# Ten activation tiles ahead in the room of four row slots, in a product-key expert kernel

## The chip, the cores and the metric

The kernel runs on one core of a Trainium2 chip. The metric is the device time of one execution in microseconds (us). The engines are named as the profile names them: PE (TensorE) with its weight loads PEld, DVE (VectorE), ACT (ScalarE), POOL (GpSimd) and SP (SyncE, which here issues most of the transfers).

## What is computed

The reference chains two blocks over 512 tokens of width 1024, in float32. Everything up to the last part (latent attention, then gated linear attention and sparse attention with top-k) is the same in both kernels and is not looked at here. The change is in the last part, a product-key expert layer (PEER) with 16384 experts:

```python
def _peer(h, w_q, sub_keys_1, sub_keys_2, expert_u, expert_v):
    q = (h @ w_q).reshape(B, S, PEER_HEADS, PEER_DKEY)
    s1, s2 = ...                                  # scores against 128 + 128 sub-keys
    v1, i1 = lax.top_k(s1, PEER_TOPK)             # 16 of each
    v2, i2 = lax.top_k(s2, PEER_TOPK)
    cand = v1[..., :, None] + v2[..., None, :]
    best, ci = lax.top_k(cand, PEER_TOPK)         # 16 of the 256 sums, for 8 heads
    expert_idx = ia * PEER_NKEYS + ib
    gates = jax.nn.softmax(best, axis=-1)
    u, v = expert_u[expert_idx], expert_v[expert_idx]
    a = gelu(einsum('td,thkd->thk', h, u)) * gates
    return einsum('thk,thkd->td', a, v)
```

## The kernel before

**Dense for three token tiles, sparse for the fourth.** Tokens come in four tiles of 128. For the first three (TD = 384 tokens) the layer is computed densely over all 16384 experts, in 128 steps j of 128 experts each. `a[j]` (128 experts x 384 tokens) is Gelu(u[j] h); `w` is a[j] times the gate matrix G, which is zero where an expert was not chosen; and w times v[j] (128 experts x 1024) adds to the result Y, which stays in six of eight PSUM banks. For the fourth tile, 128 tokens x 8 heads x 16 rows are gathered, 256 gathers of 128 rows in all: 128 of u (each reduced to one column by line 1166, output `junk`) and then 128 of v (each added into `spx` by line 1176).

**Products in three parts.** A float32 product is three matmuls: both operands are split into a rounded high part and the rest (`split`, lines 73 to 78). ACT writes the high part (`wh` from `wr` for u, from `vr` or `wr` for v, `wwh` from `w`; line 79), and DVE or POOL the rest (`wl`, `wwl`; line 81). One a tile is computed by an "a block" of 24 matmuls of 384 columns (lines 85 to 87), one step of Y by a "Y block" of 18 matmuls of 512 columns (lines 1254 to 1256). The split halves of u and v share three buffers (`wh`, `wl`, bufs=3), the raw u has two, the raw v two, w and its halves two each.

**The order of the stages.** (1) DVE chooses the experts of the first three tiles (`choose`, ending in line 1372), a long chain of 128x384 instructions. Meanwhile PE computes tiles of a ahead, with `pull`: each unit of eight is three matmuls, eight units a tile. Nineteen tiles stand here (`pull(8 * 19)`). For tiles computed ahead (`early`) the rest of the split is POOL's work. (2) PE transposes the chosen indices and gates (line 1097, output `T` by line 1099). (3) The one-hot stage: DVE and POOL write one-hot matrices `o1` and `o2` for four tokens at a time (lines 1107 and 1112), PE multiplies them (line 1125), ACT evicts the gates, and one unit of a (three matmuls) is pulled for each of 96 groups: twelve more tiles. One further tile is pulled at the end, 32 in all. (4) The expert loop, 128 steps.

**One step of the loop**, in the order of the code: `pull(8)` for the next a tile (its splits are now DVE's), `weights(j + 1)` (w, its split, the load and split of v[j + 1]), the Y block of step j, then at most two units of the fourth tile's choosing (steps 0 to 7, lines 1315 to 1378), and from step 7 on gathered rows. There are a tiles left to pull in steps 0 to 95; from step 96 on a step has only its Y block. The a tiles live in 29 buffers (NA + 1); a tile's Gelu (line 1036) waits for the w that reads the buffer's tile before.

**Gathered rows.** Eight row buffers of 128x1024 are used in turn: four in `more`, allocated when the choosing ends, and four in `rows`. `used(j)` spreads the 256 gathers over the steps 7 to 115, with three times the weight while a tiles are still pulled: two or three a step up to step 96, at most one after it.

**What sets the order.** PE follows the code's order throughout. In the loop DVE and POOL do too (`manual_schedule`). ACT's instructions and SP's transfers are put in order when the kernel is built, by a scheduler; on the chip each engine takes its instructions strictly in that order.

Of the kernel before, what the change touches and what calls it, by code (L numbers as in the profile page):

```python
# [9 lines left out]
F32 = mybir.dt.float32  # L10
# [15 lines left out]
TD = 384  # L26
NE = 16384
NA = 28
POOL_U = (3,)
POOL_A = True  # L30
LAG = 20
# [14 lines left out]
class Build:  # L46
# [961 lines left out]
    def phase_c(self, x3):  # L1008
        nc, i, tc, pc = self.nc, self.i, self.tc, self.pc
# [16 lines left out]
        def a_units(j):  # L1026

            wh, wl = au.pop(j, None) or self.wload(i["u"][j], [8, 128], early)
            ps = self.bank()
            for k in range(8):  # L1030
                self.mm3(ps[:, :TD], wh[:, k], wl[:, k], hh[:, k, :TD], hl[:, k, :TD], k == 0, k == 7)
                if k == 2 and early:
                    au[j + 1] = self.wload(i["u"][j + 1], [8, 128], True)
                yield
            a = pc.tile([128, TD], F32, name="a", tag="a", bufs=NA + 1)
            nc.scalar.activation(a, ps[:, :TD], AF.Gelu)  # L1036
            at[j] = a

# [35 lines left out]
        pr = self.es.enter_context(tc.tile_pool(name="pr", bufs=1, side="right", reuse_waits="tile"))  # L1074

        more = pr.tile([128, 4, 1024], F32, name="rows")
        early, au = True, {0: self.wload(i["u"][0], [8, 128], True)}

        def ahead():
# [5 lines left out]
        def pull(n):  # L1085
            for _ in range(n):
                next(al, None)
                self.pulled += 1

        with tc.tile_pool(name="p2", bufs=1, reuse_waits="tile") as p2:  # L1090
            ia, ib, gt = self.choose(0, NT, vals, idxs, p2)
            pull(8 * 19)
            Ts = []
            for tt in range(NT):
                ps = self.bank()
                for n, t in enumerate((ia, ib, gt)):
                    nc.tensor.transpose(ps[:, 128 * n:128 * n + 128], t[:, tt], self.ident)
                T = p2.tile([128, 3, 128], F32, name="T", tag="T", bufs=3)
                nc.scalar.activation(T, ps[:, :384].rearrange("p (n t) -> p n t", t=128), AF.Copy)
                Ts.append(T)  # L1100

            def one_hots(g):

                T, t0 = Ts[g // 32], 4 * (g % 32)
                o1 = p2.tile([128, 4, 128], F32, name="o1", tag="o1", bufs=3)
                o2 = p2.tile([128, 4, 128], F32, name="o2", tag="o2", bufs=3)
                nc.vector.tensor_tensor(o1, iota[:, None, :].to_broadcast([128, 4, 128]),
                                        T[:, 0, t0:t0 + 4].unsqueeze(2).to_broadcast([128, 4, 128]),
                                        op=OP.is_equal)
                for u in range(4):  # L1110
                    e = nc.gpsimd if u in POOL_U else nc.vector
                    e.tensor_scalar(o2[:, u], iota, T[:, 1, t0 + u:t0 + u + 1], T[:, 2, t0 + u:t0 + u + 1],
                                    op0=OP.is_equal, op1=OP.mult)
                return o1, o2

            oh = {0: one_hots(0)}
            for c in range(TD // 32):
                gb = self.xp.tile([128, 128, 32], F32, name="gb", tag="X")
                for g in range(8 * c, 8 * c + 8):
                    if g + 1 < TD // 4:  # L1120
                        oh[g + 1] = one_hots(g + 1)
                    o1, o2 = oh.pop(g)
                    ps = self.bank()
                    for u in range(4):
                        nc.tensor.matmul(ps[:, 128 * u:128 * u + 128], o1[:, u], o2[:, u], start=True, stop=True)
                    pull(1)
                    gs = 4 * (g % 8)
                    nc.scalar.activation(gb[:, :, gs:gs + 4].rearrange("p j t -> p t j"),
                                         ps.rearrange("p (t j) -> p t j", j=128), AF.Copy)
                nc.scalar.dma_start(out=gd[c], in_=gb)  # L1130
            spx = self.xp.tile([128, 4, 1024], F32, name="spx", tag="X")
            h2t, ysp, rep, fg = [spx[:, n] for n in range(4)]

            n = TD // 32 - 1
            G = {0: spx[:, 2:].rearrange("p n d -> p (n d)")[:, :4 * TD].rearrange("p (c t) -> p c t", t=128)}
            nc.sync.dma_start(out=G[0][:, :n], in_=gd[:n, :, :4].rearrange("c p j t -> p c (j t)"))
            nc.scalar.activation(G[0][:, n], gb[:, :4].rearrange("p j t -> p (j t)"), AF.Copy)
            pull(8)

        rows = self.xp.tile([128, 4, 1024], F32, name="rows", tag="X")  # L1140
        slots = [more[:, n] for n in range(4)] + [rows[:, n] for n in range(4)]
        for hf in range(2):
            ps = self.bank()
            for k in range(4):
# [5 lines left out]
        with tc.tile_pool(name="p3", bufs=1, reuse_waits="tile") as p3:  # L1150
# [3 lines left out]
            def gather(e):  # L1154

                table = i["u_rows"] if e < 128 else i["v"].rearrange("j p d -> (j p) d")
                r = slots[e % 8]
                ix = sidx[:, e // 128, e % 128:e % 128 + 1]
                nc.gpsimd.indirect_dma_start(out=r, out_offset=None, in_=table,  # L1159
                                             in_offset=bass.IndirectOffsetOnAxis(ap=ix, axis=0))  # L1160
                return e, r
# [63 lines left out]

            early = False
            NJ = NE // 128
            es, got, ready = 0, [], NJ - self.pulled // 8
            last = ready + LAG
            ch, first = choosing(), None  # L1230

            def used(j):

                share = [3 if k < ready else 1 for k in range(first, last)]
                return 256 * sum(share[:j - first]) // sum(share)
            pool_order = tc.manual_schedule(engines={mybir.EngineType.Pool, mybir.EngineType.DVE})
            pool_order.__enter__()
# [1 line left out]
            for j in range(NJ):  # L1239
                if j == 0:  # L1240
                    weights(0)
                pull(8)
                if j + 1 < NJ:
                    weights(j + 1)
                if j == NJ - 2:
                    continue
                for tt in range(NT):
                    ts_ = slice(128 * tt, 128 * tt + 128)
                    for jj in ((j,) if j < NJ - 2 else (j - 1, j)):
                        wh, wl, vh, vl = ws[jj]  # L1250
                        for n in range(2):
                            ns = slice(512 * n, 512 * n + 512)
                            y = Y[2 * tt + n]
                            nc.tensor.matmul(y, wh[:, ts_], vh[:, ns], start=(jj == 0), stop=False)  # L1254
                            nc.tensor.matmul(y, wh[:, ts_], vl[:, ns], start=False, stop=False)  # L1255
                            nc.tensor.matmul(y, wl[:, ts_], vh[:, ns], start=False, stop=(jj == NJ - 1))  # L1256
                ws.pop(j)
                for _ in range(2):
                    if first is None and next(ch, 0) == 0:
                        first = j  # L1260
                if first is not None:
                    while got and got[0][0] < used(j):
                        sparse(*got.pop(0))
                    while es < 256 and len(got) < 8:
                        got.append(gather(es))
                        es += 1
                if j == last:
                    xts = self.xp.tile([128, 4, 1024], F32, name="xts", tag="X")
                    f = i["final_g"]
                    nc.sync.dma_start(out=fg, in_=bass.AP(tensor=f.tensor, offset=f.offset, ap=[[0, 128], [1, 1024]]))  # L1270
                if 0 <= (j - last) // 2 < 4 and (j - last) % 2 == 0:
                    tt = 3 - (j - last) // 2
                    nc.sync.dma_start(out=xts[:, tt], in_=x3d[tt])
                if j == last + 2:
                    assert es == 256 and not got
                    for hf in range(2):
                        ps = self.bank()
                        for k in range(4):
                            dg = p3.tile([128, 128], F32, name="dg", tag="dg", bufs=1)
                            c = 40 + 4 * hf + k  # L1280
                            nc.vector.tensor_scalar(dg, self.ident, self.adac(c), None, op0=OP.mult)
                            nc.tensor.matmul(ps[:, 128 * k:128 * k + 128], self.ones, dg, start=True, stop=True)  # L1282
                        nc.scalar.activation(rep[:, 512 * hf:512 * hf + 512], ps, AF.Copy)
                if j == last + 4:
                    finish(3)
# [185 lines left out]
```

## Time and profile before

| | us |
|---|---|
| median of 3 runs (2253.89 to 2257.43) | 2256.93 |
| the profiled execution, its own time | 2257.13 |
| span of its trace | 2255.3 |
| PE busy in the span | 2131.9 (95%) |
| DVE busy | 1692.6 (75%) |
| ACT busy | 958.5 (42%) |
| POOL busy | 847.9 (38%) |

PE is the busiest engine, with a mean granted clock of 0.981 of full speed. Busy shares of the whole span hide that the stages have different limits, so the rows below are taken by stage. Times in them count from the span's start. In a row of the timeline the first number is the start, the second the duration; a bracket at the end says how long the engine sat idle before it and what released it. Matmuls overlap in the pipeline, so a block's length is read from start to start. `xN` at the end counts instructions merged into the row.

### The profile page before, as it was taken

To read this page: it belongs to the slowest core of one execution; us is meant where nothing else is said; L and a number is where in the kernel's file an instruction comes from. 1 tells how busy PE (TensorE), PEld (TensorE's weight loads), DVE (VectorE), ACT (ScalarE), POOL (GpSimd) and SP (SyncE) were. 2 spreads that over 40 slices of the span, in tenths; PEclk is the share of its full clock that TensorE was granted. 3 is DMA by queue.
4 is the path that set the end of the run, shared out by engine and by line. 5 is a ranking of instruction groups with operands and counts; after the bars stand their busy time and mean duration, and the time that the engine had idled before them with its cause. 6 is when DMAs were issued, how large, how long until landed. Compare 5 with 4: busy or idle time off the path is not lost. (4 is left out here: it accounts for less than half of the span.)

```text
span 2255.3 us, 31436 instructions
## 1 busy us (share of the span) xinstructions
PE 2131.9 (95%) x11443; PEld 1877.8 (83%) x11443; DVE 1692.6 (75%) x3304; ACT 958.5 (42%) x1429; POOL 847.9 (38%) x630
## 2 busy tenths in 40 slices
PE   8999999989999999999699889999999999999996
PEld 5778988877888889899688878888888888888875
DVE  6877348996667555879999678777777787877875
ACT  5376446344245533343477433333333333333332
POOL 4333330110056313335699224444444444444200
PEclk9999999999999999999899999999999999999998
DMA  6511223214822132233254659899899898899952
GB/s 249 182 48 63 79 82 112 90 57 132 274 89 66 66 107 91 93 124 120 99 202 197 227 177 333 303 322 319 307 320 312 293 319 308 309 312 309 336 184 74
DMA packets 163164, 433.08 MB, mean 192 GB/s; under 512 B 13248, under 2 KB 69952, under 8 KB 161472
## 3 DMA queue, kind: packets, MB, share of 16 engines
q1 hardware_dynamic: 121536, 267.47, 35.2%
q0 software_dynamic: 36864, 134.23, 17.2%
q10 hardware_dynamic: 4608, 29.36, 3.3%
q8 instruction: 90, 1.47, 0.3%
q14 instruction: 66, 0.54, 0.1%
HBM read 399.56 MB, written 31.46 MB: 191 GB/s over the span
## 5 line engine op out<-in xcount | busy, mean ns | idle before, releaser
L79 ACT ACTIVATE wh<-wr 128x1024 fp32r<-128x1024 f32 (+2 forms) x278 | 291.3, 1048 | 608.9 <-issue 341.0
L85 PE MATMUL bank<-h2h,wh 128*128 128x384 f32 (+2 forms) x1176 | 417.3, 355 | 22.3 <-ACT a L1036 17.5
L87 PE MATMUL bank<-h2h,wl 128*128 128x384 f32 (+2 forms) x1176 | 400.9, 341 | 4.4 <-POOL wl L81 4.4
L86 PE MATMUL bank<-h2l,wh 128*128 128x384 f32 (+2 forms) x1176 | 400.2, 340 | 0.0
L81 POOL TENSOR_TENSOR wl<-wr,wh 128x1024 fp32r<-128x1024 f32 (+2 forms) x89 | 213.9, 2407 | 414.2 <-ACT wh L79 412.0
L1255 PE MATMUL bank<-wl,wwh 128*128 128x512 f32 x768 | 302.8, 394 | 2.5 <-DVE wl L81 2.5
L1254 PE MATMUL bank<-wh,wwh 128*128 128x512 f32 x768 | 300.5, 391 | 2.3 <-ACT wwh L79 2.3
L1256 PE MATMUL bank<-wh,wwl 128*128 128x512 f32 x768 | 302.3, 394 | 0.0
L1159 POOL DMA_INDIRECT rows<-in_u_rows,sidx x128 | 176.8, 1381 | 292.4 <-DVE junk L1166 186.1
L81 DVE TENSOR_TENSOR wl<-wr,wh 128x1024 fp32r<-128x1024 f32 x189 | 233.4, 1236 | 50.5 <-ACT wh L79 49.4
L1159 POOL DMA_INDIRECT rows<-in_v,sidx x128 | 178.4, 1394 | 245.2 <-DVE spx L1176 206.0
L85 PEld LDWEIGHTS bank<-h2h,wh 128*128 128x128 f32 x1176 | 224.3, 191 | 51.8 <-ACT a L1036 43.7
L87 PEld LDWEIGHTS bank<-h2h,wl 128*128 128x128 f32 x1176 | 223.7, 190 | 9.4 <-POOL wl L81 5.3
L86 PEld LDWEIGHTS bank<-h2l,wh 128*128 128x128 f32 x1176 | 224.5, 191 | 4.9
L81 DVE TENSOR_TENSOR wwl<-w,wwh 128x384 fp32r<-128x384 f32 x128 | 71.5, 559 | 162.5 <-ACT wwh L79 162.5
L1255 PEld LDWEIGHTS bank<-wl,wwh 128*128 128x128 f32 x768 | 145.1, 189 | 32.3 <-DVE wl L81 3.7
L1254 PEld LDWEIGHTS bank<-wh,wwh 128*128 128x128 f32 x768 | 145.2, 189 | 31.1 <-ACT wwh L79 2.7
L1256 PEld LDWEIGHTS bank<-wh,wwl 128*128 128x128 f32 x768 | 145.2, 189 | 30.5
L1176 DVE SCALAR_TENSOR_TENSOR spx<-rows,coef,spx 128x1024 f32<-128x1024 f32 x127 | 162.9, 1282 | 2.5
L81 DVE TENSOR_TENSOR wl<-vr,wh 128x1024 fp32r<-128x1024 f32 x112 | 137.1, 1224 | 35.5 <-ACT wh L79 35.5
L85 PE MATMUL bank<-hh,wh 128*128 128x512 f32 (+1 forms) x408 | 160.6, 394 | 1.2 <-ACT rel L626 0.7
L1166 DVE SCALAR_TENSOR_TENSOR junk<-rows,spx 128x1024 bf16<-128x1024 f32 x128 | 156.5, 1223 | 2.8
(433 smaller groups left out, 4573.2 us busy)
## 6 DMA issues: line engine op xcount, KB each, us to landing
wr<-in_u SPq DMA_DIRECT2D x128, 512.0 KB, 5.8
vr<-in_v SPq DMA_DIRECT2D x112, 512.0 KB, 5.1
wada<-in_w_adaT SPq DMA_DIRECT2D x48, 512.0 KB, 4.3
wr<-in_w_b SPq DMA_DIRECT2D x48, 512.0 KB, 3.5
gates_d<-gb ACTq DMA_DIRECT2D x12, 2048.0 KB, 6.9
G<-gates_d SPq DMA_DIRECT2D x31, 768.0 KB, 9.5
wr<-in_w_q SPq DMA_DIRECT2D x16, 512.0 KB, 3.5
wr<-in_v SPq DMA_DIRECT2D x16, 512.0 KB, 5.3
```

What stands on the lines that cost most here:

```text
L79: nc.scalar.activation(hi, src, AF.Copy)
L81: e.tensor_tensor(lo, src, hi.bitcast(F32), op=OP.subtract)
L85: mm(ps, wh, ah, start=first, stop=False)
L86: mm(ps, wh, al, start=False, stop=False)
L87: mm(ps, wl, ah, start=False, stop=last)
L1159: nc.gpsimd.indirect_dma_start(out=r, out_offset=None, in_=table, in_offset=bass.IndirectOffsetOnAxis(ap=ix, axis=0))
L1166: nc.vector.scalar_tensor_tensor(junk, r, 1.0, h2t, op0=OP.mult, op1=OP.mult, accum_out=asp[:, e:e + 1])
L1176: nc.vector.scalar_tensor_tensor(ysp, r, coef[:, e:e + 1], ysp, op0=OP.mult, op1=OP.add)
L1254: nc.tensor.matmul(y, wh[:, ts_], vh[:, ns], start=(jj == 0), stop=False)
L1255: nc.tensor.matmul(y, wh[:, ts_], vl[:, ns], start=False, stop=False)
L1256: nc.tensor.matmul(y, wl[:, ts_], vh[:, ns], start=False, stop=(jj == NJ - 1))
```

## The change

With the change 40 tiles are computed ahead instead of 32: `pull(8 * 27)` instead of `pull(8 * 19)` beside the choosing. The tiles of the even steps 0, 2, ... 18 are written into `more`, the room of four row buffers, which holds ten of them (`spare`). All others use the 29 buffers as before. In the loop the even steps below 20 pull no tile. At step 20 the four buffers of `more` are handed to the gathers; until then these have the four of `rows`. The buffers are no longer used in turn by number but taken from a list and put back when a row has been used. `ready`, the step from which no tile is left to pull, becomes 98 (128 - 40 + 10), the last step with rows follows it, and `used` gives the weight of three only to steps 21 to 97, so that steps 7 to 20 take one row each.

```diff
+NX = 10
...
-            a = pc.tile([128, TD], F32, name="a", tag="a", bufs=NA + 1)
+            if j < 2 * NX and j % 2 == 0:
+                a = spare[:, TD * (j // 2):TD * (j // 2) + TD]
+            else:
+                a = pc.tile([128, TD], F32, name="a", tag="a", bufs=NA + 1)
             nc.scalar.activation(a, ps[:, :TD], AF.Gelu)
...
         more = pr.tile([128, 4, 1024], F32, name="rows")
+        spare = more.rearrange("p n d -> p (n d)")
...
-            pull(8 * 19)
+            pull(8 * 27)
...
-        slots = [more[:, n] for n in range(4)] + [rows[:, n] for n in range(4)]
+        slots = [rows[:, n] for n in range(4)]
...
-                r = slots[e % 8]
+                r = slots.pop(0)
...
-            es, got, ready = 0, [], NJ - self.pulled // 8
+            es, got, ready = 0, [], NJ - self.pulled // 8 + NX
...
-                share = [3 if k < ready else 1 for k in range(first, last)]
+                share = [3 if 2 * NX < k < ready else 1 for k in range(first, last)]
...
-                pull(8)
+                if not (j < 2 * NX and j % 2 == 0):
+                    pull(8)
+                if j == 2 * NX:
+                    slots += [more[:, n] for n in range(4)]
...
                     while got and got[0][0] < used(j):
+                        slots.append(got[0][1])
                         sparse(*got.pop(0))
-                    while es < 256 and len(got) < 8:
+                    while es < 256 and slots:
                         got.append(gather(es))
```

Line numbers of the changed kernel are one higher from line 29 on and four to nine higher from line 1036 on. Three places show what the change moves.

POOL at the end of the choosing, before: `wl<-wr,wh` is the rest of a split of u (the first rows are the part before, `o` the one-hots of the next stage).

```order
L138 TENSOR_TENSOR sq<-sq 128x512 x4
L138 TENSOR_TENSOR sq<-sq 128x256 x2
L81 TENSOR_TENSOR wl<-wr,wh 128x1024 x38
L1112 TENSOR_SCALAR o_10444<-iota,T 128x128
L1112 TENSOR_SCALAR o_10452<-iota,T 128x128
```

And in the changed kernel:

```order
L139 TENSOR_TENSOR sq<-sq 128x512 x4
L139 TENSOR_TENSOR sq<-sq 128x256 x2
L82 TENSOR_TENSOR wl<-wr,wh 128x1024 x46
L1117 TENSOR_SCALAR o_10698<-iota,T 128x128
L1117 TENSOR_SCALAR o_10706<-iota,T 128x128
```

Eight more splits stand ahead of the first one-hot. On PE the same place has 648 matmuls of a in a row ahead of the transposes of line 1097, 456 before. Within the one-hot stage one split of u that stood ahead of its last four instructions on POOL now stands behind them.

DVE in the loop once rows are gathered, from the w of step 10 to that of step 11, before (`G` holds the gates, `junk` is a gathered row of u, `wl<-vr` the split of v, `wl<-wr` that of u):

```order
L1187 TENSOR_TENSOR w_12961<-a_10161,G_12550 128x384
L81 TENSOR_TENSOR wwl_12964<-w_12961,wwh_12963 128x384
L81 TENSOR_TENSOR wl_12970<-vr_12967,wh_12969 128x1024
L1166 SCALAR_TENSOR_TENSOR junk_12991,asp_12178<-rows_9545,spx_12111 128x1024
L1166 SCALAR_TENSOR_TENSOR junk_12993,asp_12178<-rows_9545,spx_12111 128x1024
L1166 SCALAR_TENSOR_TENSOR junk_12995,asp_12178<-rows_12148,spx_12111 128x1024
L81 TENSOR_TENSOR wl_13005<-wr_13002,wh_13004 128x1024
L1187 TENSOR_TENSOR w_13033<-a_10194,G_12550 128x384
```

In the changed kernel, from the w of step 10 to that of step 12, two steps:

```order
L1192 TENSOR_TENSOR w_13040<-rows_9545,G_12705 128x384
L82 TENSOR_TENSOR wwl_13043<-w_13040,wwh_13042 128x384
L82 TENSOR_TENSOR wl_13049<-vr_13046,wh_13048 128x1024
L1171 SCALAR_TENSOR_TENSOR junk_13070,asp_12432<-rows_12402,spx_12365 128x1024
L1192 TENSOR_TENSOR w_13073<-a_10188,G_12705 128x384
L82 TENSOR_TENSOR wwl_13076<-w_13073,wwh_13075 128x384
L82 TENSOR_TENSOR wl_13082<-vr_13079,wh_13081 128x1024
L1171 SCALAR_TENSOR_TENSOR junk_13103,asp_12432<-rows_12402,spx_12365 128x1024
L82 TENSOR_TENSOR wl_13111<-wr_13108,wh_13110 128x1024
L1192 TENSOR_TENSOR w_13139<-rows_9545,G_12975 128x384
```

A step has one gathered row where it had three, and every second step has no split of u.

ACT around the table loads at the loop's start (the Exp of line 1336, in the choosing of the fourth tile, and the Gelu after it), from the wwh of step 3, before:

```order
L79 ACTIVATE wwh_12394<-w_12392 128x384
L79 ACTIVATE wh_12400<-vr_12398 128x1024
L79 ACTIVATE wh_12440<-wr_12438 128x1024
L1336 ACT_TABLE_LOAD
L1336 ACTIVATE gt_12433<-gt_12433 128x128
L1036 ACT_TABLE_LOAD
L1036 ACTIVATE a_12359<-bank_12284 128x384
L79 ACTIVATE wwh_12471<-w_12469 128x384
```

In the changed kernel, from the high part of v for step 4 on:

```order
L80 ACTIVATE wh_12665<-vr_12663 128x1024
L1345 ACT_TABLE_LOAD
L1345 ACTIVATE gt_12621<-gt_12621 128x128
L80 ACTIVATE wwh_12659<-w_12657 128x384
L80 ACTIVATE wh_12715<-vr_12713 128x1024
L1040 ACT_TABLE_LOAD
L1040 ACTIVATE a_12760<-bank_12632 128x384
L80 ACTIVATE wwh_12709<-w_12707 128x384
```

The high part of v for step 5 (`wh_12715`), whose buffer was that of the u of step 3, now stands ahead of the second table load, the Gelu of step 3's tile and the wwh of step 5.

## Rows read from the trace of the kernel before

**Rows 1.** Engines by stretch: choosing's end, one-hot stage, loop's start, long stretch.

```profile
core 0: us, PE busy (x) PEld busy (x) DVE busy (x) ACT busy (x) POOL busy (x), PEclk, DMA share, GB/s
1077.30:1096.00 18.70, 0.14 (x2) 0.00 (x0) 17.72 (x29) 1.00 (x1) 2.39 (x1) 0.63 0.17 57
1096.00:1253.30 157.30, 144.43 (x1075) 141.18 (x1076) 152.91 (x384) 116.96 (x122) 152.06 (x107) 0.98 0.50 192
1253.30:1347.60 94.30, 81.47 (x391) 73.80 (x390) 67.29 (x204) 31.59 (x43) 10.94 (x9) 0.93 0.54 176
1449.20:2089.40 640.20, 634.03 (x3152) 562.80 (x3151) 501.45 (x597) 223.13 (x301) 284.02 (x201) 1.00 0.90 311
```

**Rows 2.** Timeline of PE, the first transpose that waits (start, duration, instruction, [idle<-releaser]).

```profile
1096.05 0.47 PE L1097 MATMUL bank<-ident,ib 128*128 128x128 f32 x1 [18.61 <-DVE ib L1372]
```

**Rows 3.** Timeline of POOL, the last two splits ahead of the one-hot stage.

```profile
1074.22 2.75 POOL L81 TENSOR_TENSOR wl<-wr,wh 128x1024 fp32r<-128x1024 f32 x1 [1.58 <-ACT wh L79]
1078.38 2.39 POOL L81 TENSOR_TENSOR wl<-wr,wh 128x1024 fp32r<-128x1024 f32 x1 [1.40 <-ACT wh L79]
```

**Rows 4.** Timeline of DVE, one instruction of the choosing beside a split, one alone.

```profile
1074.74 2.65 DVE L1372 TENSOR_TENSOR ib<-ib,y 128x384 f32<-128x384 f32 x1
...
1081.22 0.56 DVE L1372 TENSOR_TENSOR ib<-ib,y 128x384 f32<-128x384 f32 x1
```

**Rows 5.** Timeline of PE, first matmuls of blocks in the loop (L85 a, L1254 Y).

```profile
1271.29 0.69 PE L85 MATMUL bank<-h2h,wh 128*128 128x384 f32 x1 [5.44 <-ACT a L1036]
...
1277.97 0.39 PE L1254 MATMUL bank<-wh,wwh 128*128 128x512 f32 x1
...
1347.61 0.39 PE L1254 MATMUL bank<-wh,wwh 128*128 128x512 f32 x1
...
1351.73 0.33 PE L85 MATMUL bank<-h2h,wh 128*128 128x384 f32 x1
...
1355.92 0.39 PE L1254 MATMUL bank<-wh,wwh 128*128 128x512 f32 x1
...
1449.22 0.39 PE L1254 MATMUL bank<-wh,wwh 128*128 128x512 f32 x1
...
2089.41 0.39 PE L1254 MATMUL bank<-wh,wwh 128*128 128x512 f32 x1
```

**Rows 6.** Timeline of DVE, the w of steps 0 and 8.

```profile
1253.30 2.67 DVE L1187 TENSOR_TENSOR w<-a,spx 128x384 f32<-128x384 f32 x1 [3.09 <-ACT spx L1137]
...
1332.31 0.55 DVE L1187 TENSOR_TENSOR w<-a,G 128x384 f32<-128x384 f32 x1
```

**Rows 7.** Waits of DVE from 1253.3 to 1332.4 (total us, times, longest).

```profile
DVE wwl L81 <- ACT wwh L79: 13.5, 8, 3.0
DVE wl L81 <- ACT wh L79: 3.4, 6, 1.3
```

**Rows 8.** Timeline of ACT at the loop's start: v of step 2, a table load.

```profile
1269.73 1.06 ACT L79 ACTIVATE wh<-vr 128x1024 fp32r<-128x1024 f32 x1 [6.24 <-DMA vr<-in_v]
...
1289.05 1.28 ACT L1036 ACT_TABLE_LOAD   x1
```

**Rows 9.** Timeline of DVE, w before and after three gathered rows, both halves.

```profile
1359.17 0.55 DVE L1187 TENSOR_TENSOR w<-a,G 128x384 f32<-128x384 f32 x1
...
1367.60 0.56 DVE L1187 TENSOR_TENSOR w<-a,G 128x384 f32<-128x384 f32 x1
...
1775.58 0.55 DVE L1187 TENSOR_TENSOR w<-a,G 128x384 f32<-128x384 f32 x1
...
1784.16 0.55 DVE L1187 TENSOR_TENSOR w<-a,G 128x384 f32<-128x384 f32 x1
```

**Rows 10.** Page, second part: what the transfers moved in 40 slices of 56.4 us.

```profile
GB/s 249 182 48 63 79 82 112 90 57 132 274 89 66 66 107 91 93 124 120 99 202 197 227 177 333 303 322 319 307 320 312 293 319 308 309 312 309 336 184 74
```

## The prediction, made before the changed kernel had run

> **What bounds the kernel now.** I read the table by stretch first, since a share of the whole span mixes stages with different limits. TensorE is the busy engine nearly everywhere, so the reader should look for where it is not [rows 1]. From 1077.3 to 1096.0 it does nothing: 0.14 us busy of 18.7. In the one-hot stage, 1096 to 1253, VectorE and GpSimd are full (152.9 and 152.1 of 157.3) and TensorE has some slack. At the start of the expert loop (1253 to 1348) TensorE is busy 81.5 of 94.3 at a granted clock of 0.93. In the long stretch after it, it is busy 634.0 of 640.2. The first hole has one cause [rows 2]: the transposes of the chosen indices (line 1097), which stand behind nineteen tiles of a in TensorE's order, waited 18.61 us for the last VectorE instruction of the choosing (line 1372). The holes at the loop's start come behind VectorE too, which chooses the fourth token tile there between its loop work.
>
> In these terms the change puts eight more tiles (40 units ahead for 32) into the first hole and takes eight tiles out of the loop. TensorE's work is the same; only holes can be won or opened.
>
> **The stretch of the choosing.** One tile of a is 24 matmuls; the splits for it on GpSimd follow each other at 1074.22 and 1078.38, so 4.16 us a tile, which is also TensorE's pace [rows 3]. Eight are 33.3 us. They start at 1096.05 - 18.61 = 1077.44 and end at 1110.7, so the transposes come 14.6 us later than 1096.05 on TensorE's side.
>
> VectorE's side needs a look as well, because the eight tiles bring eight more splits on GpSimd (2.4 to 2.75 us each) next to the choosing. Of VectorE's 128x384 instructions there, the one at 1074.74 took 2.65 us while a split ran, and the one at 1081.22 took 0.56 with none running [rows 3, 4]: some 2.07 us lost for each split. Seven of the new splits fall before the choosing ends, 14.5 us, which puts its end at 1110.5: within 0.2 us of TensorE's own. The Trainium skill has a rule that speaks against the change here ("SBUF — State Buffer", section "Who interferes with whom"): a VectorE instruction with two SBUF inputs and a GpSimd instruction that reads SBUF exclude each other, and whoever comes second is held for the whole instruction. The trace agrees (2.65 against 0.56); without the rule the tiles alone would set 1110.7, with it the choosing arrives at the same moment, so the sum is the same by either.
>
> The last split before the transposes came 0.9 us after the last tile's end and ran in the hole; now it falls onto the first one-hot instructions, which costs about 2.1. The order takes another split out of the one-hot stage and puts it behind the stage's last instruction, and GpSimd is full there: about -2.4 [rows 3]. So the stage's end is shifted by **+14.3**.
>
> **The start of the loop.** Steps 0, 2, ... 18 compute no tile. Price of blocks at full clock, from one free step [rows 5]: Y of step 9 starts 8.31 us after Y of step 8; of that the Y block is 1351.73 - 1347.61 = 4.12 (I use 4.15) and the a block 4.19.
>
> Up to step 8 VectorE sets the pace. Its chain from w of step 0 (1253.30) to w of step 8 (1332.31) is 79.0 us [rows 6]. Four of seven splits of u leave it, at a pitch of 1.15: -4.6. Waits in it are 13.5 + 3.4 = 16.9 [rows 7]. I rebuild these from the new order. About 3.0 at step 0 stay. At step 2 about 3.0 stay, because ScalarE still waits there for the third block of v, which landed at 1269.73 whatever VectorE did [rows 8]. At step 5 I put 3.9: ScalarE's copy of v for step 5 now stands ahead of the Gelu table load (1.28 us [rows 8]) and of that step's wwh, and waits for the a block of step 3. The other five steps are left with 0.6 each, the time of one ScalarE copy. That makes 13.1, so -3.8, and w of step 8 comes 8.4 earlier.
>
> From there the a block of step 7 waits for its split as before, at the low clock: after a hole of 5.44 us one such block took 1277.97 - 1271.29 = 6.68 for 4.19 [rows 5], which I allow for once more. In the trace Y of step 8 started 15.3 after w of step 8 with two a blocks between; now there is one, so 10.3. Together Y of step 8 comes **13.4** earlier. The bounds: if every wait of VectorE shrinks to 0.6, 22 to 23 earlier; if none of its waits shrinks and the a blocks run late, 4.6.
>
> **Steps 8 to 20.** They took 1449.22 - 1347.61 = 101.6 [rows 5]. Now they hold 12 Y blocks and 7 a blocks: 49.8 + 29.3 = 79.1. In each pair the split of u has about 4.15 us (one Y block) in which VectorE must do wwl, the split of v, one gathered row and that split, about 4.7; I add 0.3 for each of six pairs. 80.9, so **-20.7**. At no extra stall this would be -22.5.
>
> **The long stretch.** From Y of step 20 to that of the last step with a tile, 75 steps took 2089.41 - 1449.22 = 640.2 [rows 5], 8.54 a step. Now it is 77 steps. The gathered rows that steps 7 to 20 no longer take (1 a step instead of 2.67) come here: nine of ten steps have three rows, where it was two of three. A step with three rows repeats on VectorE at 8.43 in the first half and 8.58 in the second [rows 9], which is what the mean already shows, so the pace stays: 41 steps at 8.44, 36 at 8.575 and 1.5 for the change of halves, 656.2. **+16.0**. If every three-row step were to cost 0.1 more, +7.
>
> **The tail.** 31 Y blocks for 33: 2 x 4.1 = **-8.2**.
>
> Sum: 14.3 - 13.4 - 20.7 + 16.0 - 8.2 = -12.0. Against the profiled execution (2257.13 us, 0.2 above the median of the three runs, so no correction) this gives 2245. The fill of the hole (18.6) is real, but some 6 of it come back as longer holes at the loop's start.
>
> **Rivals.**
>
> *The loop's start shrinks with TensorE's work.* If ScalarE's order costs nothing, VectorE's waits fall to 0.6 a step and Y of step 8 is 22.7 earlier instead of 13.4: -21.3, 2235.8. For it: the choosing's own instructions leave gaps that a shorter step closes. Against: the in-order copies on ScalarE. Chance 0.17, from 2230 to 2239.
>
> *The loop's start gives the gain back.* Y of step 8 only 4.6 earlier, +8.8 on the sum: 2253.9, and with a late end of the choosing (one more split in its way, 2.1) 2256.0. For it: TensorE is idle for 12.8 us (94.3 - 81.5) in this place already [rows 1]. Chance 0.15, within 0.2%.
>
> *The transfers become the bound in the long stretch (slower).* A step there moves 0.524 MB each of u, v and gathered rows and 0.197 of G: 2.91 rows a step make 2.77 MB, 326 GB/s at 8.5 us, against 311 in the trace at a busy share of 0.90 [rows 1]. It decides from 317 GB/s downward: then a step takes 8.74 and 77 of them cost over 17 us, more than the sum gains. At 311 it is 8.91 a step, +28, 2273. Against it: one slice reached 336 GB/s [rows 10], and the rows name no wait for a transfer in this stretch. Chance 0.09.
>
> *The clock stays low at the loop's start.* Here the clock was 0.93 with TensorE 86% busy [rows 1]; with fewer a blocks it is busy some 65%. With every block of steps 0 to 7 at half speed, 8 x 8.3 + 4 x 8.4 = 100 us instead of some 74: +26, 2271. By the Trainium skill ("TensorE: Matmul & The Clock Gate", section "HAM oscillation — how this bites in real kernels") repeated holes can hold the array at its slow clock. In the trace the block after the 5.44 us hole lost 2.5 us [rows 5], yet the stretch as a whole kept 0.93 [rows 1]. Chance 0.04.
>
> That the change does nothing is excluded by the order: TensorE has 648 matmuls of a in a row ahead of the transposes instead of 456.
>
> **How the numbers follow.** The forecast of 2245 (2239 to 2252) has 0.55. Faster by over 0.2%, which is about what a measurement of this kernel can tell from no change and means below 2252.4: 0.55 + 0.17 = 0.72. Within 0.2%: 0.15. Slower: 0.13. The range from 2233 to 2258 leaves out the two slow cases and the far end of the first rival.
>
> **What would show it.** Right: the transposes start at about 1111 with hardly any wait, and VectorE instructions of 2.6 us appear every 4.16 us until then; the one-hot stage lasts 157 us again; from w of step 0 to Y of step 8 it takes about 81 us (94.3 before) with a wait of over 2 us at step 5; steps 21 to 97 run at 8.4 to 8.6. Wrong: the choosing ends past 1115; or the waits at the loop's start differ by more than 5 us from 13; or the long stretch leaves 8.54 a step, or TensorE waits for a transfer in it.

## The result: 2235.0 us, and where the time went

The changed kernel takes 2235.0 us (median of 4 runs, 2233.57 to 2240.27), the one before in the same comparison 2256.36: a ratio of 0.9911, 95% interval 0.9893 to 0.9929, 21.4 us faster. The profiled execution has a span of 2231.7 us against 2255.3, PE is busy 2120.1 us (95%), DVE 1693.0 (76%), at a mean granted clock of 0.982. The forecast was 2245 with a range of 2233 to 2258: sign and range held, the middle was 10 us too slow.

The stretches of the changed kernel, in the columns of [rows 1] (choosing's end, one-hot stage, loop's start, long stretch):

```profile
1075.50:1108.60 33.10, 33.10 (x193) 33.10 (x192) 32.13 (x29) 11.43 (x16) 20.37 (x8) 1.00 0.39 127
1108.60:1265.50 156.90, 142.56 (x1072) 139.12 (x1071) 152.69 (x385) 117.48 (x125) 154.40 (x107) 0.99 0.51 194
1265.50:1348.90 83.40, 63.45 (x277) 55.79 (x276) 55.68 (x194) 24.61 (x33) 6.75 (x5) 0.86 0.50 165
1428.60:2068.30 639.70, 639.70 (x3237) 582.44 (x3236) 530.49 (x645) 224.88 (x309) 301.25 (x220) 1.00 0.94 332
```

The hole beside the choosing is filled (33.1 of 33.1). The loop's start is shorter, though TensorE is idle there for more of it (20 of 83 us, 12.8 of 94 before) and at a lower clock (0.86, 0.93 before). The long stretch takes as long as before but holds 77 steps instead of 75, and TensorE never stops in it.

Stage by stage, read from the first waiting transpose, w of step 0, and the first Y matmul of steps 8, 20 and the last with a tile:

| | forecast | measured |
|---|---|---|
| choosing and one-hot stage, to w of step 0 | +14.3 | +12.2 (1253.3 to 1265.5; the stages ahead of the choosing came 1.8 earlier, so +14.0) |
| w of step 0 to Y of step 8 | -13.4 | -10.9 (94.3 to 83.4) |
| steps 8 to 20 | -20.7 | -21.9 (101.6 to 79.7) |
| long stretch | +16.0 | **-0.6** (640.2 for 75 steps, 639.6 for 77) |
| tail | -8.2 | **-2.5** (165.9 to 163.4) |
| sum | -12.0 | -23.7 (spans: -23.6) |

Two terms are off, in opposite directions: a step of the long stretch takes 8.31 us instead of 8.54, and the tail gave a third of what it should.

### The profile page after: what moved, and what is told of

Same layout as the page of the kernel before. It is cut to its first block, busy times and chain, and to the rows that moved or that the text cites. A ratio compares the mean times of both kernels' runs of the same rounds, so it can differ in the third digit from the quotient of the medians.

```text
span 2231.7 us, 31519 instructions
## 1 busy us (share of the span) xinstructions
PE 2120.1 (95%) x11443; PEld 1882.8 (84%) x11443; DVE 1693.0 (76%) x3296; ACT 952.2 (43%) x1429; POOL 858.1 (38%) x638
## 3 DMA queue, kind: packets, MB, share of 16 engines
q0 software_dynamic: 36864, 134.23, 16.9%
## 4 chain that ended last, share of the span: by engine, by line
PE 72%; DVE 15%; issue 5%; ACT 4%; DMA 3%; POOL 1%; ACTq 0%; DVEq 0%; SPq 0%; POOLq 0%
PE bank L88 15%; PE bank L87 15%; PE bank L86 15%; PE bank L1263 7%; PE bank L1264 7%; PE bank L1262 7%; DVE o L1117 2%; DVE wl L82 1%; DVE o L1112 1%; DMA wada<-in_w_adaT 1%; DVE sel L844 1%; DVE m L843 1%; ACT wh L80 1%; DVE junk L276 1%; DVE rstd L111 1%
## 5 line engine op out<-in xcount | busy, mean ns | idle before, releaser
L86 PE MATMUL bank<-h2h,wh 128*128 128x384 f32 (+2 forms) x1176 | 410.1, 349 | 2.9 <-ACT wh L80 2.9
L82 POOL TENSOR_TENSOR wl<-wr,wh 128x1024 fp32r<-128x1024 f32 (+2 forms) x97 | 234.2, 2418 | 422.9 <-ACT wh L80 420.9
L1164 POOL DMA_INDIRECT rows<-in_u_rows,sidx x128 | 171.6, 1340 | 308.4 <-DVE junk L1171 209.8
L1164 POOL DMA_INDIRECT rows<-in_v,sidx x128 | 173.5, 1356 | 211.5 <-DVE spx L1181 177.7
L82 DVE TENSOR_TENSOR wl<-wr,wh 128x1024 fp32r<-128x1024 f32 x180 | 222.3, 1235 | 40.7 <-ACT wh L80 39.1
L80 ACT ACTIVATE wwh<-w 128x384 fp32r<-128x384 f32 x128 | 66.8, 522 | 259.1 <-PE bank L1263 238.1
```

The costliest lines, as they stand in the source:

```text
L80: nc.scalar.activation(hi, src, AF.Copy)
L82: e.tensor_tensor(lo, src, hi.bitcast(F32), op=OP.subtract)
L86: mm(ps, wh, ah, start=first, stop=False)
```

## The theories

**A, the lead.** Before, 32 tiles are computed ahead in 29 buffers, so in step j the Gelu of tile j + 31 needs the buffer that w of step j + 2 reads. It stands on ACT between that w and its rounded half `wwh`, for which DVE waits. With ten tiles in the spare room the Gelu of step j needs the buffer of tile j, whose w stands a step earlier in the code and is done by then. Then the long stretch gains from the buffers, not from tiles computed ahead.

**B, the dealing out.** The changed shares of gathered rows, or the room itself, make the 8.31.

**C, DVE's order, against D, loads and ACT.** At the loop's start three a blocks wait for the split of their u, which DVE does behind the choosing of the step before. These waits should go if that order changes (C) or move to another place (D).

All kernels below ran against the kernel before, whose median was 2256.3, 2255.8 and 2256.4 in the three groups of runs. Kernels with the same code up to the loop differ by up to 7 us at w of step 0 (1264.3 and 1271.5 in e5 and f1 below), and runs of one kernel by up to 9. Most of the 7 us lies ahead of the part that the change touches: the first tile of a starts at 987.9 us in e5 and at 993.6 in f1. From there to w of step 0 the six kernels with the changed code up to the loop take 276.1 to 277.9 us and the kernel before takes 262.0, so the change costs 14 to 16 us there. So beside the medians I read stages from the traces:

| | tiles ahead | w of step 0 | to Y of step 20 | a step after it | last block's Y to the end | median us |
|---|---|---|---|---|---|---|
| before | 32 | 1253.3 | 195.9 | 8.536 | 165.9 | 2256.4 |
| e2_before_share | 32 | 1252.5 | 192.6 | 8.532 | 166.2 | 2253.5 |
| e1_before_30 | 30 | 1244.0 | 186.9 | 8.307 | 157.5 | 2230.3 |
| e8_30_slow | 30 | 1249.2 | 175.5 | 8.307 | 160.4 | 2228.8 |
| nx2 | 32 | 1248.1 | 187.3 | 8.307 | 159.0 | 2236.5 |
| nx5 | 35 | 1255.0 | 183.5 | 8.307 | 164.1 | 2243.8 |
| changed kernel | 40 | 1265.5 | 163.1 | 8.307 | 163.4 | 2235.0 |
| e3_after_42 | 42 | 1275.4 | 234.6 | 8.531 | 168.1 | 2318.7 |
| e5_after_xts_pool | 40 | 1264.3 | 163.4 | 8.307 | 156.7 | 2231.2 |
| e4_after_slow_choosing | 40 | 1269.8 | 153.0 | 8.307 | 159.0 | 2224.3 |
| f1_after_u_first | 40 | 1271.5 | 152.6 | 8.307 | 160.2 | 2224.0 |
| f2_slow_u_first | 40 | 1267.4 | 140.6 | 8.307 | 159.3 | 2210.4 |
| f3_slow_u_first_xts | 40 | 1266.5 | 141.2 | 8.307 | 158.3 | 2206.9 |

The long stretch is 77 steps, 75 where a step takes over 8.5.

## Experiments on the long stretch

**e1_before_30**, the kernel before with two tiles fewer ahead:

```diff
-            pull(8 * 19)
+            pull(8 * 17)
```

> The kernel before with two activation tiles fewer ahead (30 instead of 32), nothing else. In the kernel before, the long stretch goes at 8.54 us a step (75 steps), in the changed one at 8.31 (77 steps). Theory A (the lead): with 32 tiles ahead and 29 buffers, a tile's Gelu waits for the w of the next step on DVE, and that closes a ring of gathered rows, split, w, Gelu, bank, next block; with 30 tiles the Gelu needs a buffer that the step before gave back, so no Gelu waits for DVE and the steps take 8.31. Sum: choosing about 3.6 us earlier (two tiles of 1.8), two more steps with a block instead of without (+8.3), 75 steps 0.23 us shorter (-17): about 2244 us. Theory B (the pace is DVE's own, or comes from how the rows are dealt out): steps stay at 8.5 and the time is about 2261 us.

2230.3 us, ratio 0.9889 (0.9872 to 0.9905): one number taken down by two brings at least as much as the whole change, and 14 us more than I expected of A. The step of 8.31 came as expected; the rest is that w of step 0 came 9.3 us earlier instead of 3.6 (2.6 of it in the stages ahead of the first tile of a) and that w of step 0 to Y of step 20 took 9.0 less, which I had not counted. First what stood before the Gelu (line 1036) on ACT, for the kernel before and then for e1:

```profile
its engine sat idle before it (us, times) until:
  DVE w L1187: 211.8, 94
  PE bank L87: 2.9, 2
```

```profile
its engine sat idle before it (us, times) until:
  PE bank L87: 2.8, 2
```

94 Gelus waited for a w, and then none. What that did to DVE shows in one step with three gathered rows, timelines of ACT and DVE, before and then e1:

```profile
1776.16 0.49 ACT L1036 ACTIVATE a<-bank 128x384 f32<-128x384 f32 x1 [2.87 <-DVE w L1187]
1776.55 0.52 ACT L79 ACTIVATE wwh<-w 128x384 fp32r<-128x384 f32 x1
...
1777.10 0.56 DVE L81 TENSOR_TENSOR wwl<-w,wwh 128x384 fp32r<-128x384 f32 x1 [0.97 <-ACT wwh L79]
```

```profile
1774.92 0.55 DVE L1187 TENSOR_TENSOR w<-a,G 128x384 f32<-128x384 f32 x1
...
1775.60 0.53 ACT L79 ACTIVATE wwh<-w 128x384 fp32r<-128x384 f32 x1 [2.58 <-PE bank L1255]
...
1776.16 0.56 DVE L81 TENSOR_TENSOR wwl<-w,wwh 128x384 fp32r<-128x384 f32 x1 [0.69 <-ACT wwh L79]
...
1780.86 0.47 ACT L1036 ACTIVATE a<-bank 128x384 f32<-128x384 f32 x1
...
1783.23 0.55 DVE L1187 TENSOR_TENSOR w<-a,G 128x384 f32<-128x384 f32 x1
```

Before, ACT does the Gelu between w (1775.58, [rows 9]) and `wwh`, and DVE waits 0.97 for both. In e1 the Gelu comes five microseconds after w, DVE waits 0.69, and from w to w it is 1783.23 - 1774.92 = 8.31 instead of 8.58. The 0.28 us between the two waits are the whole difference (0.27), and 8.31 is TensorE's own step: 639.70 of 639.70 us busy.

```profile
1430.90:2070.60 639.70, 639.70 (x3237) 582.44 (x3236) 510.90 (x608) 224.99 (x309) 283.03 (x203) 1.00 0.91 316
```

**e2_before_share**, the kernel before with the new dealing out of rows:

```diff
-                share = [3 if k < ready else 1 for k in range(first, last)]
+                share = [3 if 20 < k < ready else 1 for k in range(first, last)]
```

> The kernel before with only the change's dealing out of the gathered rows: up to step 20 one row a step instead of three, then the 24 rows are spread over the long stretch. Theory A (the lead): the long stretch stays at 8.5 us a step; steps 8 to 20, with fewer rows on DVE, may gain 0 to 3 us; 2253 to 2257 us. Theory B (the dealing out of the rows makes the 8.31): the long stretch goes to 8.31, about 2239 us.

2253.5 us, ratio 0.9987 (0.9978 to 0.9997). The step stays at 8.53, so the shares do not make the 8.31, and e1 has no spare room: B falls with the two together. The shares gain 3 us, at the loop's start.

**e3_after_42**, the changed kernel with two more tiles ahead, so that the Gelu runs two steps short of buffers again:

```diff
-            pull(8 * 27)
+            pull(8 * 29)
```

> The changed kernel with two more tiles ahead (42 instead of 40): from step 20 a tile's Gelu again needs the buffer that the w of a later step gives back, as in the kernel before; rows, spare room and skipped blocks stay. Theory A (the lead): the long stretch goes back to about 8.5 us a step (75 steps, +17 us against 8.31), two steps fewer have a block (-8.3), the choosing's stretch grows by 3.6 to 8.3: 2247 to 2252 us. Theory B (spare room and dealing out make the 8.31): it stays there, and the time is 2230 to 2235 us.

2318.7 us, ratio 1.0276 (1.0259 to 1.0293). The long stretch did what A says (8.531), but I had not thought of the loop's start. There the pairs of steps take 20.48 us instead of 12.63, and w of step 0 to Y of step 20 is 71 us longer. PE and ACT in one such pair:

```profile
1439.84 0.69 PE L86 MATMUL bank<-h2h,wh 128*128 128x384 f32 x1 [5.47 <-ACT a L1040]
...
1439.30 0.49 ACT L1040 ACTIVATE a<-bank 128x384 f32<-128x384 f32 x1 [3.38 <-DVE w L1192]
```

Where every second step has no block, the w that frees the buffer is four steps on instead of two, and a later block waits on TensorE for the Gelu to free its bank: 5.47 us a pair. The two stretches up to Y of steps 8 and 20, with a granted clock of 0.75 and 0.86:

```profile
1275.40:1389.80 114.40, 66.76 (x270) 58.35 (x270) 57.75 (x194) 24.02 (x32) 6.20 (x5) 0.75 0.37 122
1389.80:1510.00 120.20, 91.96 (x387) 81.18 (x386) 49.60 (x69) 28.86 (x39) 19.11 (x16) 0.86 0.49 160
```

**nx2**, two tiles in the spare room and 32 ahead, as many as before:

```diff
-NX = 10
+NX = 2
-            pull(8 * 27)
+            pull(8 * 19)
```

> The changed kernel with two tiles in the spare room instead of ten, and 32 ahead, as many as in the kernel before: it differs from that one in the Gelu's buffers alone, from the dealing out of rows apart. Theory A (lead): buffers for 31 Gelus, so none waits for DVE's w; the long stretch goes at 8.31 (-17 us), the waits for ACT's Gelu at the loop's start go (some -5 to -10): 2226 to 2232 us. Rival (32 ahead is too many, or the ten tiles of the change are what brings the gain): 2250 to 2256 us.

2236.5 us, ratio 0.9917 (0.9897 to 0.9936), with 77 steps at 8.307: the same gain as the whole change within its uncertainty, though no tile more is computed ahead than in the kernel before. It is 4.5 us over the upper end for A: the waits at the loop's start did not shrink, they changed their cause (5.4, 1.7 and 3.0 us for DVE's split, where the Gelu was waited for).

**nx5**, five in the room and 35 ahead (`NX = 5`, `pull(8 * 22)`).

> The changed kernel with five tiles in the spare room and 35 ahead. By the two ends that were run (30 ahead without spare room 2230.3, 40 ahead with ten 2235.0): if each tile more ahead delays the choosing's end by 1.8 us and saves 4.15 us of a step that TensorE bounds, five give -11.8 against 30 ahead, 2219 us; if the skipped blocks only turn into waits for DVE at the loop's start, as it seems with ten, 2230 to 2235 us. Between them 2224 us is expected.

2243.8 us, ratio 0.9934 (0.9913 to 0.9956), a miss: I took the middle of two ends, and it lies outside both. From w of step 0 to the end it takes 987.2 us against 984.0 in e1, although five blocks (some 21 us) have left the loop. Four of them left during the choosing and became the same three waits as with ten (5.4, 5.5 and 6.4 us), and the tail is 6.6 us longer than in e1. With ten, it is the blocks of steps 8 to 18 that pay.

## Experiments on the loop's start and the tail

In the changed kernel these are the three waits, with the first Y matmul after the first of them, and what DVE did ahead of the first (`gt` is a piece of the fourth tile's choosing):

```profile
1297.86 0.69 PE L88 MATMUL bank<-h2h,wl 128*128 128x384 f32 x1 [5.27 <-DVE wl L82]
...
1303.70 0.39 PE L1262 MATMUL bank<-wh,wwh 128*128 128x512 f32 x1
...
1317.90 0.69 PE L88 MATMUL bank<-h2h,wl 128*128 128x384 f32 x1 [5.49 <-DVE wl L82]
...
1339.05 0.69 PE L88 MATMUL bank<-h2h,wl 128*128 128x384 f32 x1 [6.39 <-DVE wl L82]
...
1296.40 0.27 DVE L1344 TENSOR_TENSOR gt<-best 128x128 f32<-128x128 f32 x1
1296.58 1.22 DVE L82 TENSOR_TENSOR wl<-wr,wh 128x1024 fp32r<-128x1024 f32 x1
```

Each costs more than its own length. The 22 matmuls left of the first block took 1303.70 - 1297.86 = 5.84 us, where 22/24 of 4.19 is 3.84: 2 us more, at a mean granted clock of 0.64, between the lower level (1.2 GHz) and the full one (2.4 GHz). In the columns of [rows 1]:

```profile
1297.80:1303.70 5.90, 5.84 (x22) 5.84 (x23) 4.18 (x22) 0.52 (x1) 0.00 (x0) 0.64 0.51 178
```

**e4_after_slow_choosing**, one piece of the fourth tile's choosing a step:

```diff
-                for _ in range(2):
+                for _ in range(1):
                     if first is None and next(ch, 0) == 0:
```

> The changed kernel with the fourth tile's choosing spread over twice as many steps: one piece a step instead of two, so it ends at step 15 instead of 7, and the gathered rows begin there. Theory C (DVE's order sets the loop's start: two pieces of choosing a step stand ahead of the split that the next block waits for, three PE waits of 5.3, 5.5 and 6.4 us): these 17 us shrink to near zero and the pairs of steps go at 12.6 us from the start; from step 0 to 20 some 145 us instead of 163, about 2218 us. Rival D (the start is held by loads of v, 7.2 us in one wait, and by ACT's order and its table loads): the waits stay in other places, 2230 to 2235 us, and the later rows cost a little in the long stretch.

2224.3 us, ratio 0.9863 (0.9846 to 0.9879): 10.7 us under the changed kernel, two thirds of what C expected. Five waits of 1.4 to 2.2 us stay, because DVE still does the next step's choosing ahead of the split. **e8_30_slow** is the same edit on e1, where no step lacks a block:

> The kernel before with 30 tiles ahead and the fourth tile's choosing at one piece a step, so no tile in a spare room and no step without a block. Theory C (DVE's choosing holds the loop's start): TensorE's four waits there (2.4, 1.7, 3.0 and 0.2 us) go, 2223 us. If it comes out at or under the 2224.3 of the changed kernel with slow choosing, the ten tiles bring nothing of their own; if they are worth their 23 us (ten blocks of 4.15 saved, 18 paid in the choosing), it stays some 20 us above that, which 2223 already denies.

2228.8 us, ratio 0.9879 (0.9857 to 0.9900). Here TensorE has no wait left at the loop's start:

```profile
1249.20:1325.00 75.80, 75.80 (x397) 69.85 (x396) 45.55 (x135) 31.57 (x43) 2.41 (x1) 1.00 0.60 201
```

From w of step 0 to Y of step 20 it gained 11.4 us on e1; the median moved by 1.6, since this kernel came to step 0 5.2 us later with the same code and its tail was 2.9 longer (holes of 2.0 and 1.2 us). So ten tiles ahead were worth some 4 us at that point (2224.3 against 2228.8), less than the 9 us by which the runs of e8 alone differ.

**f1_after_u_first** moves the load and split of the next u ahead of the choosing in a step without a block:

```diff
                     weights(j + 1)
+                n = self.pulled // 8
+                if j < 2 * NX and j % 2 == 0 and n not in au:
+                    au[n] = self.wload(i["u"][n], [8, 128])
```

> The changed kernel with one thing moved: in the steps without a block, the load and split of the next block's u are written ahead of that step's choosing instead of at the block itself, behind it. Theory C (DVE's order holds the loop's start): the three waits of a block for its split on DVE (5.3, 5.5, 6.4 us) go; then DVE's sum sets the pace: two steps hold 5.9 us of splits and products, about 1.3 us of waits for ACT and 7.8 us of choosing, 15 us instead of 21, so -15 to -18 us with the clock that comes back, 2217 to 2220 us. Rival D (loads of v or ACT's order hold it, or DVE has too much to do in any order): 2230 to 2236 us.

2224.0 us, ratio 0.9858 (0.9842 to 0.9875), 4 us over the range for C. The three waits became 3.1, 7.1 and 0.2 us, and w of step 0 to Y of step 20 fell from 163.1 to 152.6. Order is part of it. The rest is the sum of DVE's work beside two pieces a step: in the 23.3 us up to the end of the 7.1 us wait DVE is busy for 20.7.

**f2_slow_u_first** has both edits.

> The same move on the changed kernel with slow choosing, whose start still showed TensorE waiting five times for the split (1.7, 1.4, 2.2, 2.0, 2.1 us) and a lower clock after each. Theory C: all five go, and with the clock some 12 to 15 us, about 2210 us; then ten tiles more ahead are worth about 18 us against the kernel with 30 ahead and slow choosing (2228.8), near the 23 that ten blocks of 4.15 us less 18 us of longer choosing make. Rival (the rest is the first step's start and loads): 2220 to 2225 us, and the ten tiles are worth hardly anything.

2210.4 us, ratio 0.9801 (0.9785 to 0.9817), as C expected, though two of the five waits are left (1.6 and 0.4 us). Its loop's start and the long stretch:

```profile
1267.40:1327.00 59.60, 56.80 (x277) 50.10 (x276) 35.79 (x122) 24.69 (x34) 2.39 (x1) 0.97 0.63 210
...
1408.00:2047.60 639.60, 639.60 (x3236) 582.34 (x3235) 539.41 (x661) 224.95 (x309) 310.36 (x228) 1.00 0.95 338
```

59.6 us from w of step 0 to Y of step 8, 83.4 in the changed kernel, with the same matmuls; the clock is 0.97 again. Now ten tiles ahead are worth 18 us by the medians (2210.4 against the 2228.8 of e8): step 0 begins 18.2 later and the loop is 36.0 shorter. Some 3 of the 18 are not theirs, since f2 came to its first tile of a 2.8 us earlier, through stages that are the same in both: 15 are.

**e5_after_xts_pool** is for the tail. SP's transfers in the changed kernel, then the copy of v on ACT that was late and the two holes on PE:

```profile
2068.27 0.80 SPq L1282 DMA_DIRECT2D xts<-x_d  x2
2071.11 0.37 SPq L1189 DMA_DIRECT2D G<-gates_d  x1
2071.52 2.00 SPq L1282 DMA_DIRECT2D xts<-x_d  x1
2074.66 3.18 SPq L92 DMA_DIRECT2D wr<-in_v  x1
2077.89 0.43 SPq L1282 DMA_DIRECT2D xts<-x_d  x1
...
2090.65 1.06 ACT L80 ACTIVATE wh<-wr 128x1024 fp32r<-128x1024 f32 x1 [7.18 <-DMA wr<-in_v]
...
2092.17 0.50 PE L1262 MATMUL bank<-wh,wwh 128*128 128x512 f32 x1 [2.65 <-ACT wwh L80]
2093.90 0.77 PE L1263 MATMUL bank<-wl,wwh 128*128 128x512 f32 x1 [1.23 <-DVE wl L82]
```

The code has the four `xts` loads (512 KB each) in steps 118 to 124. The scheduler put them on SP as soon as the last a block gave back their buffer, at 2068, beside the last gathers. A load of v between them (issued from 2074.66 on) landed 15.9 us after its issue began; the median of that kind of load in this kernel is 5.5.

```diff
-                    nc.sync.dma_start(out=xts[:, tt], in_=x3d[tt])
+                    nc.gpsimd.dma_start(out=xts[:, tt], in_=x3d[tt])
```

> The changed kernel with the four loads of xts (512 KB each) issued from GpSimd's queue at their written place, steps 118 to 124, instead of from SyncE's, where they stand in a row at 2068 to 2078 us, ahead of a load of v. Theory T (that load comes late because of them): TensorE's holes at 2081 to 2094 us (0.3, 2.7 and 1.2 us) go, -4 us, about 2231 us. Rival (the gathers and G hold the load): the holes stay, 2235 us.

2231.2 us, ratio 0.9890 (0.9874 to 0.9907), as T expected; the stretch from the last block on is 156.7 instead of 163.4. On POOL, which keeps the code's order, the loads come after the last gather, and the load of v is not waited for:

```profile
2126.91 2.19 POOL L1282 DMA_DIRECT2D xts<-x_d  x4
...
2084.53 1.06 ACT L80 ACTIVATE wh<-wr 128x1024 fp32r<-128x1024 f32 x1 [2.01 <-PE bank L1264]
```

**f3_slow_u_first_xts** joins it to f2.

> The same with the four loads of xts on GpSimd's queue. If the late load of v costs the tail 1 to 4 us there as in the changed kernel: 2206 to 2209 us, 1 to 4 us under the kernel without this edit; if the tail of the kernel with slow choosing was already free of it (its holes were 0.3 and 0.7 us): the same time.

2206.9 us, ratio 0.9782 (0.9764 to 0.9799), the fastest kernel run here, 28 us under the changed one. Against f2 the edit brings 1.0 us in the tail (158.3 against 159.3); the rest of the 3.5 between the medians is within their intervals. The same load of v landed after 8.4 us here and after 12.7 in f2, which speaks for the xts loads as what delays it. But their place on SP does not by itself open a hole: e1, nx2, e4, f1 and f2 keep it, and no wait of TensorE around that load is longer than 0.9 us there. In the kernel before, where all four are issued within 2 us, the load landed after 8.1 us. What makes the difference was not tested.

## Why the forecast was right in sign and off in size

**The choosing: right.** The transposes came when TensorE had done its tiles, and VectorE was held by the splits until the same moment: its last instruction ends at 1108.80. PE's first transpose, and DVE's last two instructions of the choosing:

```profile
1108.63 0.27 PE L1102 MATMUL bank<-ident,ia 128*128 128x128 f32 x1
...
1105.57 0.56 DVE L1379 SCALAR_TENSOR_TENSOR y<-cf,step 128x384 f32<-128x384 f32 x1
1106.16 2.64 DVE L1381 TENSOR_TENSOR ib<-ib,y 128x384 f32<-128x384 f32 x1
```

1108.63 against 1111, less the 1.8 by which all came earlier; 2.64 us beside a split, as in [rows 4]. The rule of the Trainium skill that was weighed here ("SBUF — State Buffer", section "Who interferes with whom") held: both sides arrived together. The one-hot stage is 156.9 us, as forecast. From the first tile of a to w of step 0 it is 14.1 us more than before (276.1 against 262.0), for a forecast of 14.3.

**The loop's start: right in kind.** -10.9 for -13.4. That VectorE's order sets it is what e4, f1 and f2 confirm. The late wwh at step 5 is in the trace of the changed kernel, and so is its reason, ACT's copy of v that waits for an a block:

```profile
1303.77 1.06 ACT L80 ACTIVATE wh<-vr 128x1024 fp32r<-128x1024 f32 x1 [4.89 <-PE bank L87]
...
1308.41 0.56 DVE L82 TENSOR_TENSOR wwl<-w,wwh 128x384 fp32r<-128x384 f32 x1 [5.75 <-ACT wwh L80]
```

The sizes were off: VectorE's waits up to w of step 8 add up to 18.4 us (18.0 for wwh, 0.4 for wh), where 13.1 was forecast, 5.75 instead of 3.9 at step 5 and 5.8 instead of 3.0 at step 0. That is more than 5 us from 13, one of the forecast's own signs of being wrong. It cost less than that, mostly because w of step 0 took 0.56 us instead of the 2.67 of [rows 6]; from w of step 0 to w of step 8 it took 73.4 us, where 70.6 was forecast and 79.0 was measured before. Steps 8 to 20 came within 1.2 us.

**The long stretch: the step that failed.** The term was +16.0, on the ground that "a step with three rows repeats on VectorE at 8.43 in the first half and 8.58 in the second" and "so the pace stays". That took the pitch of [rows 9] for VectorE's own, although it contained a wait of 0.97 us for `wwh`, and behind that a Gelu which waited for a buffer. The change removes that dependence as a side effect. The measured term is -0.6: 77 steps at 8.307, TensorE's pace, 16.6 less than forecast. That the step would leave 8.54 was another of the forecast's own signs of being wrong.

**The tail: mis-sized.** -8.2 assumed that 31 Y blocks run as 33 did, and where no late load opens a hole they do: the tail of e1 is 157.5 (-8.4), that of e5 156.7 (-9.2). In the changed kernel the holes of 2.65 and 1.23 us behind the late load of v, and a granted clock of 0.85 in the 11 us after them (1.00 in e5), gave back about 6.

**The range: held in part by luck.** With the long stretch as it was measured and all else as forecast the sum gives 2228.5 us, below the range's lower end of 2233. The tail and the loop's start, which gave less than forecast, brought the time back into it.

**The rivals.** 2235.8 was the time of the first rival, but not by its mechanism: the waits at the loop's start did not shrink to 0.6 each (83.4 us, not some 72). Its 22.7 is also 1 us more than its own terms give: eight waits of 0.6 for 16.9 save 12.1, and with 4.6 and 5.0 that is 21.7. The transfers did not become the bound: 332 GB/s at a busy share of 0.94, and 338 in f2, without a TensorE wait. The low clock at the loop's start did show (0.86), with the waits and not in every block. The Trainium skill's remark on repeated holes that was set beside that rival ("TensorE: Matmul & The Clock Gate", section "HAM oscillation — how this bites in real kernels") fits e3 more, where holes of 5 to 17 us came in every pair of steps and the granted clock was 0.75 and then 0.86; it was 1.00 as soon as they ended.

So the gain of the change is mostly that of having buffers for what is computed ahead (nx2), and 30 tiles ahead without any spare room gain as much or more (e1). The eight tiles that it computes ahead beyond those of nx2 bring step 0 some 17 us later and shorten the loop by 20 (985.9 to 966.2 from w of step 0 to the end); they pay only once VectorE's order lets the loop's start use them (f2). That two more buffers alone would do it in the kernel before was not tried.

## What to carry to other kernels

Count the buffers of work computed ahead at the instruction that writes them: two short, that instruction waits for a later consumer and turns up inside that consumer's own chain. Before a step's length is taken as an engine's own pace, subtract the waits in it and ask which of them the change touches. And a hole that is filled ahead pays only where the place from which the work is taken was bound by that engine: there, see what stands on the other engines' queues ahead of the next operand.

## What was not expected of the hardware

A hole of 5.3 us on TensorE cost 7.3, since the 22 matmuls after it took 5.84 us instead of 3.84, at a granted clock of 0.64. With three holes of 5.3 to 6.4 us the mean over 83 us was 0.86; with them gone (f2) it was 0.97.

The transfer engines at a share of 0.95 and 338 GB/s over 640 us (f2) never made TensorE wait. Beside gathers and four loads of 512 KB, issued within 10 us, a single 512 KB load took 15.9 us to land in the changed kernel, against a median of 5.5 for that kind of load; with the four elsewhere it took 8.4 (f3, against 12.7 in f2).
